# RWKV-7 head pairs: solver and preparation of the next pair moved into the running pair's chain, transposes over 128 partitions

## The chip, the core and the metric

The kernel runs on one core of a Trainium2 chip. The metric is the device time of one execution in microseconds (us), median of three runs. All matrix work runs on TensorE (PE), whose weight loads are listed apart (PEld); the elementwise work is spread over VectorE (DVE), ScalarE (ACT) and GpSimd (POOL), and SyncE (SP) issues the DMAs.

## What is computed

The program is a trunk of two layers. Each layer normalises x (512 tokens by 1024), projects it, runs four mixers on it (Mamba-2 SSD, RWKV-7, differential attention, grouped-query attention), projects their joined output back, normalises and adds. The change lies in the RWKV-7 mixer alone. Its core, per head and direction, is a recurrence over tokens:

```python
def step(S, inp):
    r_t, w_t, k_t, v_t, a_t, b_t = inp
    sa = jnp.einsum("bhvk,bhk->bhv", S, a_t)
    S = S * w_t[:, :, None, :] + sa[..., None] * b_t[:, :, None, :] + v_t[..., None] * k_t[:, :, None, :]
    return S, jnp.einsum("bhvk,bhk->bhv", S, r_t)
...
wkv = wkv_f + flip(wkv_b)
```

There are 8 heads of 64 channels, and one scan runs forwards and one backwards over the 512 tokens. Each layer also computes:

```python
mix = jnp.einsum("ble,ed->bld", jnp.concatenate([y_a, y_b, y_c, y_d], axis=-1), w_out[i])
x = x + _rms_norm(mix, post_norm_w[i])
```

## The kernel before

**Stages.** A layer runs in order: pre-norm and a low-rank projection; `prep(0)`, the preparation of the first head pair; the RWKV-7 stage with its four head pairs j; then SSD and the output projection. In the trace the RWKV-7 stage of the first layer is 100.5 to 676 us, that of the second 1019 to 1592 us.

**A head pair.** Two heads lie on the two halves of the 128 partitions. The 512 tokens are 8 chunks of 64; within a chunk the recurrence is solved as a 64x64 triangular system, and from chunk to chunk a 64x64 state is carried. Both directions d run side by side. The steps of a pair, in program order:
- `products(j)`: the 64x64 products of r and a against k and b (tile `pa`), masked into `AT` by DVE. Before, both m (k or b) are computed in one loop, and the two halves e go to output half `e ^ m`, so all four quadrants (input half by output half) of the PE array are used.
- `turned(j)`: V transposed by 64x64 products with the identity (`p`, line 82), and b with k transposed two at a time by PE (`pt`, line 452), evicted by ACT into `V2` and `BKT`.
- the solver: the 16x16 diagonal blocks of the system are brought side by side by four DVE stream transposes of 32 partitions by 512 (line 528), inverted in 15 steps of two small DVE instructions (lines 541, 543), and put back by eight more stream transposes (lines 549, 551) into `DN` and `DT`; three rounds of PE products with a DVE addition each (`ch`, `TT`, line 571) make the inverse `TT`.
- products that the chain needs: `px` (into `AT[0]`), `pk` (into `KV`) and `py` (the part of the output that needs no state, into `Y0`).
- the chain over 8 chunks, cc: from the state `St` the product `bk` row 0, then DVE adds `Xs`, then `bk` row 1 with `TT`, then DVE copies `Us`, then `bk` row 2 and DVE makes the new state `S`; outputs accumulate in the PSUM tile `yb`. These are three hops between PE and DVE in each chunk, 24 in a pair.
- `norm(j)`: group norm and gate of the finished pair.

**What goes in between.** `fill(us)` lets attention work (projections `pjt`, `pjc`, scores `sc`, softmax, `ptp`, `ob`) run in the amount of `us` times a scale that spends the same total in each layer. `ahead()` takes one step of a list of generators: `turned(j)`, `norm(j - 1)`, `prep(j + 1)`. Both are called between the solver's steps (`F_SV`, `F_MG`) and between the chain's hops (`F_CH`). `products(j + 1)` run inside the chain, from the fourth chunk on. A scheduler then orders the instructions of each engine; every engine works its own list in order.

The call that paces a hop of the chain, and the pacing scale, are:

```python
fill.scale = END * 299.5 / (4 * (15 * F_SV + 5 * F_MG + 24 * F_CH) + F_GN)
ahead()
fill(F_CH)
```

`prep(j)` (line 333 on) issues about 13 DVE instructions of 128x512 for each direction, the ACT exponentials and logarithms, and the small PE products `p`, among them `block_mm`, which has ACT make `bh` and POOL make `bl` first (lines 283, 284).

Of the kernel before, what the change touches and what calls it, by code (L numbers as in the profile page):

```python
# [10 lines left out]
F32 = mybir.dt.float32  # L11
# [8 lines left out]
L = 512  # L20
# [7 lines left out]
F_SV = 1.5  # L28
F_MG = 2.4
F_CH = 1.7  # L30
# [7 lines left out]
C_LAG = 4  # L38
N_PR = 3
# [36 lines left out]
def trunk(ctx: ExitStack, tc: tile.TileContext, x_in, win, wwd, wdt, wout, w2a, cols, rows, sscal, consts, out, dbg=None,  # L76
# [175 lines left out]
    def rwkv(i, lay, pw, ps, rp, fill):  # L252
# [63 lines left out]
        def prep(j):  # L316
# [18 lines left out]
            for d in range(2):  # L335
# [79 lines left out]
        BKT = rp.tile([128, 2, 2, 8, 64], F32, tag="BKT", name="BKT")  # L415
        V2 = rp.tile([128, 2, 8, 64], F32, tag="V2", name="V2")

        ba = AT[0][:, :, :, 0, :]
        half = [slice(0, 64), slice(64, 128)]

        def products(j, c0, n):

            ar = AR[:, j % 2:j % 2 + 3:2]
            for d in range(2):
                BK = sts[j]["BK"][d][:, 64:].rearrange("p (c a t) -> p c a t", c=8, a=2)
                pa = [ps.tile([128, n, 128], F32, tag="g", name="pa") for _ in range(2)]
# [5 lines left out]
                for m in range(2):
                    V.tensor_tensor(AT[m][:, d, c0:c0 + n].rearrange("p c a t -> p c (a t)"), pa[m],
                                    rmask.unsqueeze(1).to_broadcast([128, n, 128]), op=ALU.mult)

        def turned(j):
            BK, v = sts[j]["BK"], sts[j]["v"]
            for d in range(2):

                p5 = ps.tile([128, 8, 64], F32, tag="g", name="p5")  # L440
                for cc in range(8):
                    for e in range(2):
                        mm(p5[half[1 - e], cc, :], v[d][half[e], cc * 64:cc * 64 + 64], ident[half[e], half[e]], True, True)
                S.activation(V2[:, d], p5, AF.Copy)
                yield
            for d in range(2):
                for e in range(2):
                    pt = ps.tile([128, 8, 64], F32, tag="g", name="pt")

                    n = 7 + e  # L450
                    for cc in range(n):
                        PE.transpose(pt[:, cc, :], BK[d][half[e], (2 * cc + 1 - e) * 64:(2 * cc + 3 - e) * 64],
                                     ident[half[e], half[e]])
                    S.activation(BKT[:, d, e, 0:n], pt[:, 0:n], AF.Copy)
                    yield
# [47 lines left out]
        fill.scale = END * 299.5 / (4 * (15 * F_SV + 5 * F_MG + 24 * F_CH) + F_GN)  # L503
        products(0, 0, 4)
        products(0, 4, 4)
        ys = None
        for j in range(4):
            Aa, Ar, lamC = (sts[j][n] for n in ("a", "r", "lamC"))
            ahead.gens = [turned(j)]
# [7 lines left out]
            sv = rp.tile([128, 1024], F32, tag="sv", name="sv", bufs=1)  # L517
            As = sv[:, 0:512].rearrange("p (t s) -> p t s", t=16)
            As2 = sv[:, 512:768].rearrange("p (t s) -> p t s", t=16)
            Ti = sv[:, 768:1024].rearrange("p (t s) -> p t s", t=16)  # L520
            DT = rp.tile([128, 2, 8, 64], F32, tag="dt", name="DT", bufs=1)
            DN = rp.tile([128, 2, 8, 64], F32, tag="dn", name="DN", bufs=1)
            G.memset(sv[:, 768:1024], 0.0)
            G.memset(sv[:, 768:1024:17], 1.0)
            quad = [(slice(32 * q, 32 * q + 32), slice(32 * (q % 2), 32 * (q % 2) + 32)) for q in range(4)]
            unit = lambda t, q: t[quad[q][0], :, :, quad[q][1]].rearrange("p d c (h t) -> p t h (d c)", h=2)
            for q in range(4):
                V.transpose(out=As[quad[q][0]].rearrange("p t (h s) -> p t h s", h=2), in_=unit(ba, q))
            V.scalar_tensor_tensor(As2, As[:, :, 0:16], th[0], As[:, :, 16:32], op0=ALU.mult, op1=ALU.add)

            bam = AT[0].rearrange("p d c a t -> p (d c) a t")[:, :, 0, :]
            G.tensor_tensor(bam, bam, nomask.unsqueeze(1).to_broadcast([128, 16, 64]), op=ALU.mult)
            G.memset(DT, 0.0)
            G.memset(DN, 0.0)
            for jj in range(15):
                ahead()
                fill(F_SV)
                n = 15 - jj
                ot = rp.tile([128, 64], F32, tag="ot", name="ot", bufs=1)
                o3 = ot[:, 0:n * (jj + 1)].rearrange("p (a b) -> p a b", a=n)  # L540
                V.tensor_tensor(o3, As2[:, jj + 1:16, jj:jj + 1].to_broadcast([128, n, jj + 1]),
                                Ti[:, jj:jj + 1, 0:jj + 1].to_broadcast([128, n, jj + 1]), op=ALU.mult)
                V.tensor_tensor(Ti[:, jj + 1:16, 0:jj + 1], Ti[:, jj + 1:16, 0:jj + 1], o3, op=ALU.add)

            Dx = sv[:, 0:512].rearrange("p (t h s) -> p t h s", t=16, h=2)
            for h in range(2):
                V.tensor_scalar(Dx[:, :, h, :], Ti, th[h], None, op0=ALU.mult)
            for q in range(4):
                V.transpose(out=unit(DN, q), in_=Dx[quad[q][0]].rearrange("p t h s -> p s h t"))
            for q in range(4):  # L550
                V.transpose(out=unit(DT, q), in_=Dx[quad[q][0]])
            ahead()
            fill(F_MG)
            chd = lambda d: ps.tile([128, 8, 64], F32, tag=f"ch{d}", name=f"ch{d}")
            both = [(cc, e) for cc in range(8) for e in range(2)]

            Mp = rp.tile([128, 2, 8, 64], F32, tag="sv", name="Mp", bufs=1)
            for d in range(2):
                pm = chd(d)
                for cc, e in both:  # L560
                    mm(pm[half[e], cc, :], ba[half[e], d, cc, :], DN[half[e], d, cc, :], True, True)
                S.activation(Mp[:, d], pm, AF.Copy)
            TT = rp.tile([128, 2, 8, 64], F32, tag="dn", name="TT", bufs=1)
            for n in range(3):
                ahead()
                fill(F_MG)
# [865 lines left out]
```

## Time and profile before

| | us |
|---|---|
| median of three runs | 1852.17 (1848.23 to 1852.95) |
| profiled execution | 1854.4 |
| its span, first to last instruction | 1852.6 |
| PE busy in the span | 1642.2 (89%) |
| DVE busy | 1163.1 (63%) |
| ACT busy | 810.5 (44%) |
| POOL busy | 698.9 (38%) |

The mean granted TensorE clock is 0.939 of full speed. Read it stage by stage: PE busy and the other engines' busy time in each stretch, then what PE waits for. Durations come from the profiled execution; in the profile a matrix product of float32 operands appears as two records, and records overlap, so the time of a row of products is taken from start to start.

### The profile page before, as it was taken

How to read it: one execution, taken by the hardware profiler on the slowest of the kernel's cores; microseconds unless marked ns; L12 is line 12 of the kernel's file. 1: busy time of each engine (PE TensorE's matmuls, PEld its weight loads, DVE VectorE, ACT ScalarE, POOL GpSimd, SP SyncE). 2: the span in 40 equal slices, each digit the busy share in tenths (PEclk: the TensorE clock that was granted, in tenths of full speed). 3: DMA queues.
4: the chain of work that ended last, by engine and by line, in shares of the span. 5: the costliest groups of instructions: out<-in, count | busy, mean ns of one | idle time of the engine just before them, and what ended most of it. 6: DMA issues, size and time to landing. Idle time of an engine off the chain costs nothing. (4 is left out here: it accounts for less than half of the span.)

```text
span 1852.6 us, 35939 instructions
## 1 busy us (share of the span) xinstructions
PE 1642.2 (89%) x14616; PEld 1325.0 (72%) x14616; DVE 1163.1 (63%) x2426; ACT 810.5 (44%) x1566; POOL 698.9 (38%) x728
## 2 busy tenths in 40 slices
PE   7887989998988999988897799899889898999888
PEld 6576767776767877766785677687677677778666
DVE  4587586676665437886256865956856744378852
ACT  4644245435524255442346442563444242554431
POOL 4443233334242334543354332433432323345333
PEclk9898999999989999989999989999999899999899
DMA  4111101111001114122431111011110011231223
GB/s 152 60 40 39 35 24 42 49 41 44 26 24 47 42 54 135 64 73 88 134 104 52 32 39 36 29 37 50 37 44 30 24 47 36 81 112 53 86 86 114
DMA packets 57510, 108.41 MB, mean 59 GB/s; under 512 B 6784, under 2 KB 8832, under 8 KB 57344
## 3 DMA queue, kind: packets, MB, share of 16 engines
q1 hardware_dynamic: 57344, 106.11, 17.7%
q8 instruction: 114, 1.87, 0.4%
q14 instruction: 52, 0.43, 0.1%
HBM read 95.60 MB, written 10.49 MB: 57 GB/s over the span
## 5 line engine op out<-in xcount | busy, mean ns | idle before, releaser
L144 POOL TENSOR_TENSOR wlo<-wf,whi 128x512 fp32r<-128x512 f32 x228 | 315.6, 1389 | 444.7 <-ACT whi L143 360.2
L82 PE MATMUL pjt<-whi,hhi 128*128 128x256 f32 x960 | 297.5, 310 | 13.0 <-ACT raw L269 6.5
L82 PE MATMUL pjt<-wlo,hhi 128*128 128x256 f32 x960 | 293.7, 307 | 1.1 <-POOL wlo L144 1.1
L82 PE MATMUL pjt<-whi,hlo 128*128 128x256 f32 x960 | 287.9, 300 | 0.0
L143 ACT ACTIVATE whi<-wf 128x512 fp32r<-128x512 f32 x228 | 141.3, 628 | 215.8 <-PE pjt L82 104.0
L82 PEld LDWEIGHTS pjt<-whi,hhi 128*128 128x128 f32 x960 | 192.6, 201 | 34.6 <-issue 9.0
L82 PEld LDWEIGHTS pjt<-wlo,hhi 128*128 128x128 f32 x960 | 192.6, 201 | 11.4 <-issue 6.5
L82 PEld LDWEIGHTS pjt<-whi,hlo 128*128 128x128 f32 x960 | 193.0, 201 | 8.8 <-issue 5.6
L82 PE MATMUL pjc<-hhi,whi 128*128 128x512 f32 x384 | 161.8, 421 | 9.0 <-ACT raw L269 5.2
L82 PE MATMUL pjc<-hhi,wlo 128*128 128x512 f32 x384 | 159.7, 418 | 0.0
L82 PE MATMUL pjc<-hlo,whi 128*128 128x512 f32 x384 | 158.1, 412 | 0.0
L872 DVE TENSOR_REDUCE nm<-sc 128x1 f32<-128x512 f32 x96 | 65.9, 687 | 84.6 <-PE sc L82 78.1
L875 ACT ACTIVATE p<-sc,nm 128x512 f32<-128x512 f32 x96 | 65.9, 686 | 115.1 <-DVE nm L872 114.7
L82 PE MATMUL mix<-whi,ylo 128*128 128x512 f32 x256 | 106.1, 414 | 5.4 <-DVE ylo L1216 5.4
L82 PE MATMUL sc<-qT,qT 64*128 64x512 f32 (+1 forms) x256 | 101.7, 494 | 7.2 <-ACT y L1055 3.8
L82 PE MATMUL mix<-whi,yhi 128*128 128x512 f32 x256 | 101.0, 417 | 5.1 <-ACT yhi L1215 5.1
L82 PE MATMUL mix<-wlo,yhi 128*128 128x512 f32 x256 | 104.4, 408 | 0.0
L82 PEld LDWEIGHTS pjc<-hhi,whi 128*128 128x128 f32 x384 | 76.5, 199 | 32.9 <-issue 6.6
L82 PEld LDWEIGHTS pjc<-hhi,wlo 128*128 128x128 f32 x384 | 76.3, 199 | 21.4 <-issue 4.2
L82 PEld LDWEIGHTS pjc<-hlo,whi 128*128 128x128 f32 x384 | 76.5, 199 | 15.7 <-issue 0.3
L1224 POOL TENSOR_TENSOR wlo<-wf,whi 128x512 fp32r<-128x512 f32 x32 | 44.4, 1390 | 112.3 <-ACT whi L1223 107.6
L1223 ACT ACTIVATE whi<-wf 128x512 fp32r<-128x512 f32 x64 | 40.4, 631 | 94.0 <-PE mix L82 59.3
(331 smaller groups left out, 3828.6 us busy)
## 6 DMA issues: line engine op xcount, KB each, us to landing
wf<-in_win_dram SPq DMA_DIRECT2D x224, 256.0 KB, 2.9
wf<-in_wout_dram SPq DMA_DIRECT2D x64, 256.0 KB, 2.6
y<-y_dram SPq DMA_DIRECT2D x24, 256.0 KB, 2.7
xt<-in_x_dram SPq DMA_DIRECT2D x8, 512.0 KB, 4.0
y_dram<-y SPq DMA_DIRECT2D x16, 256.0 KB, 2.7
y_dram<-rs SPq DMA_DIRECT2D x8, 256.0 KB, 2.1
x_dram<-t SPq DMA_DIRECT2D x8, 256.0 KB, 2.4
xt<-x_dram SPq DMA_DIRECT2D x4, 512.0 KB, 4.3
```

Source lines behind the costliest of these rows:

```text
L82: PE.matmul(o, lhsT, rhs, start=start, stop=stop, skip_group_check=skip)
L143: S.activation(hi, wf, AF.Copy)
L144: G.tensor_tensor(lo, wf, hi.bitcast(F32), op=ALU.subtract)
L872: V.tensor_reduce(nm, sc, axis=AX, op=ALU.max, negate=True)
L875: S.activation(p, sc, AF.Exp, bias=nm, accum_out=sm)
L1223: S.activation(hi, wf, AF.Copy)
L1224: (V if kt % 2 else G).tensor_tensor(lo, wf, hi.bitcast(F32), op=ALU.subtract)
```

## The change

It does these things in the RWKV-7 stage; nothing else in the program is changed.
- `solve(j)` is a generator of 31 steps that holds the products with b of pair j, the solver, and the transposes of V and k. `solve(0)` runs by itself after `prep(0)`. For j of 1 to 3 it follows `prep(j)` in the list of `ahead`, so that it runs inside the chain of pair j - 1. `ahead(2 + (n == 0))` takes two or three steps a hop.
- `bulk(j)` (12 steps) stands between the chains: the products with k, `px`, the transposes of b (`BT`), `KV`, and the part of the output that needs no state, which now accumulates into `yb` directly. `Y0` and `py` fall away, and `ys` becomes an ACT copy.
- All 64x64 products read and write the same half, so that two of the four quadrants are used. V, k and b are each transposed by 64x64 products with the identity, 768 in the program in place of 256 for V and 240 `pt` transposes.
- The stream transposes: four ACT copies bring the blocks into one tile, one DVE stream transpose of 128x512 turns it, three times a pair in place of twelve of 32x512. Over the program that is 96 of 32x512 out, 24 of 128x512 and 96 ACT copies of 32x512 in. The evictions of `pa` are all 128x512, 64 of them, in place of 88 of mixed sizes.
- The pacing constants: `F_SV` 0.7, `F_BU` 0.8, `F_CH` 2.3, `F_C3` 3.0 (last pair), with the same total.

The core of the diff:

```diff
-F_SV = 1.5
-F_MG = 2.4
-F_CH = 1.7
+F_SV = 0.7
+F_BU = 0.8
+F_CH = 2.3
+F_C3 = 3.0
...
+        quad = [(slice(32 * q, 32 * q + 32), slice(32 * (q % 2), 32 * (q % 2) + 32)) for q in range(4)]
+        unit = lambda t, q: t[quad[q][0], :, :, quad[q][1]].rearrange("p d c (h t) -> p t h (d c)", h=2)
+        both = [(cc, e) for cc in range(8) for e in range(2)]
+        bank = lambda nm: ps.tile([128, 8, 64], F32, tag="g", name=nm)
+        clear = lambda o: mm(o, cr[:, 272:273].to_broadcast([128, 128]), hT["hi"][:, 0, :], True, True)
+        rev = lambda d, cc: slice((7 * d + (1 - 2 * d) * cc) * 64, (7 * d + (1 - 2 * d) * cc) * 64 + 64)
+
+        def products(j, m):
 
             ar = AR[:, j % 2:j % 2 + 3:2]
+            to = AT[(j + m) % 2]
             for d in range(2):
+                BK = sts[j]["BK"][d]
+                for c0 in (0, 4):
+                    pa = ps.tile([128, 4, 128], F32, tag="g", name="pa")
+                    for cc in range(4):
                         for e in range(2):
+                            mm(pa[half[e], cc, :].rearrange("p (a t) -> p a t", a=2), BK[half[e], c0 + cc, m, :],
                                ar[half[e], :, d, c0 + cc, :], True, True)
...
+        def turned(src, to, d):
+
+            pt = bank("pt")
+            for cc, e in both:
+                mm(pt[half[e], cc, :], src(cc)[half[e]], ident[half[e], half[e]], True, True)
+            S.activation(to[:, d], pt, AF.Copy)
...
+        def solve(j):
+            yield from products(j, 0)
+            s = sts[j]
+            ba = AT[j % 2][:, :, :, 0, :]
+            sv = rp.tile([128, 1024], F32, tag="sv", name="sv", bufs=1)
+            As = sv[:, 0:512].rearrange("p (t s) -> p t s", t=16)
+            As2 = sv[:, 512:768].rearrange("p (t s) -> p t s", t=16)
+            Ti = sv[:, 768:1024].rearrange("p (t s) -> p t s", t=16)
+            DT = rp.tile([128, 2, 8, 64], F32, tag="dt", name="DT", bufs=1)
+            DN = rp.tile([128, 2, 8, 64], F32, tag="dn", name="DN", bufs=2)
+            s["TT"] = DN
+            close = DT[:, 0].rearrange("p c t -> p (c t)")
+            G.memset(DN, 0.0)
+            thu = lambda t, q: t[quad[q][0]].rearrange("p (t h u) -> p t h u", t=16, h=2)
+            for q in range(4):
+                S.activation(thu(close, q), unit(ba, q), AF.Copy)
+            yield
+            V.transpose(out=sv[:, 0:512], in_=close)
+            V.scalar_tensor_tensor(As2, As[:, :, 0:16], th[0], As[:, :, 16:32], op0=ALU.mult, op1=ALU.add)
+            G.memset(sv[:, 768:1024], 0.0)
+            G.memset(sv[:, 768:1024:17], 1.0)
+            G.memset(DT, 0.0)
...
+            for to, view in ((DN, "p t h s -> p s h t"), (DT, None)):
+                close = sv[:, 512:1024]
+                V.transpose(out=close.rearrange("p (t h s) -> p t h s", t=16, h=2), in_=Dx.rearrange(view) if view else Dx)
+                for q in range(4):
+                    S.activation(unit(to, q), thu(close, q), AF.Copy)
+                yield
...
+            s["V"] = rp.tile([128, 2, 8, 64], F32, tag="sv", name="VT", bufs=1)
+            s["K"] = rp.tile([128, 2, 8, 64], F32, tag="dt", name="KT", bufs=1)
+                turned(lambda cc: s["v"][d][:, cc * 64:cc * 64 + 64], s["V"], d)
+                yield
+                turned(lambda cc: s["BK"][d][:, cc, 1, :], s["K"], d)
+                yield
...
+        def bulk(j):
+            s = sts[j]
+            VT, KT, ba, ka = s["V"], s["K"], AT[j % 2][:, :, :, 0, :], AT[1 - j % 2]
+            yield from products(j, 1)
+            for d in range(2):
+                px = bank("px")
+                for cc, e in both:
+                    mm(px[half[e], cc, :], ka[half[e], d, cc, 0, :], VT[half[e], d, cc, :], True, True)
+                S.activation(ba[:, d], px, AF.Copy)
+                yield
+            for d in range(2):
+                turned(lambda cc: s["BK"][d][:, cc, 0, :], BT, d)
+                yield
+            s["KV"] = KV = rp.tile([128, 2, 8, 64], F32, tag="kv", name="KV", bufs=1)
+            for d in range(2):
+                pk = bank("pk")
+                for cc, e in both[:14]:
+                    mm(pk[half[e], cc, :], KT[half[e], d, cc, :], VT[half[e], d, cc, :], True, True)
+                V.tensor_tensor(KV[:, d, 0:7], pk[:, 0:7, :], s["lamC"][:, d, 0:7].unsqueeze(2).to_broadcast([128, 7, 64]),
+                                op=ALU.mult)
+                yield
+            s["yb"] = yb = ps.tile([128, L], F32, tag="yb", name="yb")
+            clear(yb)
+            for d in range(2):
+                for cc, e in both:
+                    mm(yb[half[e], rev(d, cc)], VT[half[e], d, cc, :], ka[half[e], d, cc, 1, ::1 - 2 * d], False, True, True)
+                yield
...
-        fill.scale = END * 299.5 / (4 * (15 * F_SV + 5 * F_MG + 24 * F_CH) + F_GN)
-        products(0, 0, 4)
-        products(0, 4, 4)
+        fill.scale = END * 299.5 / (30 * F_SV + 48 * F_BU + 72 * F_CH + 24 * F_C3 + F_GN)
+        for _ in solve(0):
+            fill(F_SV)
...
+            for _ in bulk(j):
+                fill(F_BU)
...
-                ahead.gens.append(prep(j + 1))
+                ahead.gens += [prep(j + 1), solve(j + 1)]
+            def step(n):
+                ahead(2 + (n == 0))
+                fill(F_CH if j < 3 else F_C3)
...
-            V.tensor_tensor(ys, yb, Y0, op=ALU.add)
+            S.activation(ys, yb, AF.Copy)
```

DVE while the inverse of the first pair is finished, before (`thw`, `lr`, `cs`, `AR`, `rn`, `lk`, `b`, `BK`, `rk` are prep(1); `DN`, `DT` and `sv` the solver):

```order
L549 STREAM_TRANSPOSE DN<-sv 32x16x2x16 x2
L347 TENSOR_SCALAR thw<-thw 128x512
L261 SCALAR_TENSOR_TENSOR lr<-raw,cols,lt 128x512
L353 SCALAR_TENSOR_TENSOR cs<-cst,thw 128x128 x4
L549 STREAM_TRANSPOSE DN<-sv 32x16x2x16 x2
L551 STREAM_TRANSPOSE DT<-sv 32x16x2x16 x4
L375 TENSOR_TENSOR AR<-lr,lam 128x512
L374 SCALAR_TENSOR_TENSOR rn<-lk,cols,rn 128x512
L384 TENSOR_TENSOR lk<-ka,lk 128x512
L387 TENSOR_TENSOR AR<-rn,lam 128x512
```

The same place of the changed kernel (`solve(0)`; `nm`, `rs`, `r`, `p` are the softmax of attention, `KV` belongs to `bulk(0)`):

```order
L483 TENSOR_SCALAR sv<-sv,cst 128x16x16 x2
L486 STREAM_TRANSPOSE sv<-sv 128x512
L862 TENSOR_REDUCE nm<-sc 128x1
L486 STREAM_TRANSPOSE sv<-sv 128x512
L867 RECIPROCAL rs<-sm 128x1
L1021 SCALAR_TENSOR_TENSOR r_1418<-rs,nlam,sm 128x1
L1022 SCALAR_TENSOR_TENSOR p<-p,r_1418 128x512
L503 TENSOR_TENSOR DN<-ph,DT 128x512 x6
L433 TENSOR_TENSOR AT_435<-pa,cst 128x512 x4
L532 TENSOR_TENSOR KV<-pk,lamC 128x448 x2
```

No instruction of prep(1) stands here any more; eight transposes have become two.

DVE in the first pair's chain, around the second chunk, before (`Xs`, `Us`, `S` are the chain):

```order
L389 SCALAR_TENSOR_TENSOR b_1838<-tha,rn 128x512
L384 TENSOR_TENSOR lk<-ka,lk 128x512
L872 TENSOR_REDUCE nm<-sc 128x1
L390 SCALAR_TENSOR_TENSOR BK<-b_1838,il 128x8x64
L624 TENSOR_TENSOR Xs_1788<-bk_1769,AT_434 128x64
L624 TENSOR_TENSOR Xs_1792<-bk_1772,AT_434 128x64
L877 RECIPROCAL rs<-sm 128x1
L263 SCALAR_TENSOR_TENSOR lv<-raw,cols,lt 128x512
L1031 SCALAR_TENSOR_TENSOR r_1705<-rs,nlam,sm 128x1
L635 COPY Us_1815<-bk_1769 128x64
```

The same chunk of the changed kernel:

```order
L1022 SCALAR_TENSOR_TENSOR p<-p,r_1677 128x512
L374 TENSOR_TENSOR AR<-lr,lam 128x512
L373 SCALAR_TENSOR_TENSOR rn<-lk,cols,rn 128x512
L381 TENSOR_TENSOR lk<-ka,lk 128x512
L384 TENSOR_TENSOR AR<-rn,lam 128x512
L386 SCALAR_TENSOR_TENSOR b_1804<-tha,rn 128x512
L387 SCALAR_TENSOR_TENSOR BK<-b_1804,il 128x8x64
L397 SCALAR_TENSOR_TENSOR rk<-lr,cols,lk 128x512
L260 SCALAR_TENSOR_TENSOR lv<-raw,cols,lt 128x512
L262 SCALAR_TENSOR_TENSOR lk<-raw,cols,lt 128x512
L308 SCALAR_TENSOR_TENSOR gate<-gate,pjc 128x512
L626 COPY Us_1919<-bk_1792 128x64
```

Ten instructions of prep(1) that stood ahead of the chain, and some behind its first chunk, now stand in a row between this chunk's `Xs` and its `Us`.

## Rows read from the trace of the kernel before

**Rows 1.** Windows, RWKV-7 stage of both layers: start:end, length, busy us (instructions) of PE, PEld, DVE, ACT, POOL, then granted clock, DMA share, GB/s.

```profile
100.50:676.00 575.50, 516.94 (x5775) 416.01 (x5774) 372.31 (x839) 245.02 (x483) 195.57 (x190) 0.94 0.12 37
1019.00:1592.00 573.00, 515.57 (x5765) 416.20 (x5764) 371.20 (x837) 243.30 (x479) 194.27 (x189) 0.93 0.12 37
```

**Rows 2.** Windows, first layer: four solver stretches, two of four chains, sum of all eight.

```profile
113.30:173.40 60.10, 47.35 (x661) 37.95 (x660) 49.27 (x81) 31.01 (x50) 17.84 (x21) 0.89 0.10 32
...
237.50:320.20 82.70, 73.01 (x822) 58.12 (x820) 64.05 (x124) 45.53 (x81) 32.77 (x28) 0.96 0.11 34
320.20:385.50 65.30, 64.38 (x664) 49.63 (x665) 38.30 (x99) 25.97 (x50) 21.65 (x25) 1.00 0.15 48
385.50:467.40 81.90, 69.52 (x807) 58.19 (x803) 60.57 (x103) 40.27 (x69) 33.59 (x27) 0.92 0.12 40
467.40:545.80 78.40, 70.55 (x707) 56.55 (x710) 50.90 (x143) 31.03 (x78) 26.29 (x29) 0.91 0.09 28
545.80:619.40 73.60, 66.45 (x832) 55.57 (x830) 37.78 (x80) 31.74 (x69) 17.89 (x16) 0.95 0.11 37
...
sum 559.80, PE 502.22 PEld 404.41 DVE 364.67 ACT 240.63 POOL 187.90; mean PE 62.78 PEld 50.55 DVE 45.58 ACT 30.08 POOL 23.49
```

**Rows 3.** Waits of PE in 100.5 to 676 us: in total us, times, longest.

```profile
PE p L82 <- ACT bh L283: 15.4, 4, 10.9
PE bk L82 <- DVE Xs L624: 8.4, 2, 4.5
```

**Rows 4.** Timeline around the longest wait: start, us, engine, instruction, count [idle before].

```profile
137.83 4.30 DVE L551 STREAM_TRANSPOSE DT<-sv 32x512 f32<-32x512 f32 x4
...
142.16 0.69 DVE L375 TENSOR_TENSOR AR<-lr,lam 128x512 f32<-128x512 f32 x1
...
150.64 0.80 PE L82 MATMUL p<-bh,cr 128*128 128x512 f32 x1 [10.94 <-ACT bh L283]
```

**Rows 5.** Timeline in the third pair's chain.

```profile
522.69 5.52 DVE L997 SCALAR_TENSOR_TENSOR gqk<-gqk,grr,arow 128x128 f32<-128x128 f32 x12 [2.06 <-POOL grr L126]
...
529.08 0.48 PE L82 MATMUL bk<-Xs,TT 64*64 64x64 f32 x4 [4.50 <-DVE Xs L624]
```

**Rows 6.** Window just behind the longest wait.

```profile
150.60:155.00 4.40, 4.36 (x16) 1.86 (x18) 2.07 (x3) 3.05 (x6) 2.66 (x4) 0.50 0.15 51
```

**Rows 7.** Groups of DVE instructions, whole program: count, busy us, mean ns.

```profile
L549 DVE STREAM_TRANSPOSE DN<-sv 32x512 f32<-32x512 f32 x32 | 38.7, 1209 | 1.3 <-DVE sv L547 0.5
L551 DVE STREAM_TRANSPOSE DT<-sv 32x512 f32<-32x512 f32 x32 | 34.4, 1074 | 0.6
L528 DVE STREAM_TRANSPOSE sv<-AT 32x512 f32<-32x512 f32 x32 | 33.8, 1057 | 0.4
...
L715 DVE TENSOR_TENSOR su<-su,sdt 64x512 f32<-64x512 f32 x2 | 1.4, 682 | 0.0
```

**Rows 8.** Groups of ACT instructions, whole program.

```profile
L258 ACT ACTIVATE lt<-raw,dv 128x512 f32<-128x512 f32 x52 | 37.3, 720 | 26.3 <-DVE BK L390 12.8 <-DVE lk L384 7.7 <-POOL bl L284 3.2
...
L444 ACT ACTIVATE V<-p 128x512 f32<-128x512 f32 x16 | 9.5, 596 | 28.5 <-PE p L82 28.5
```

**Rows 9.** Timeline of PE: transposes of V, then of b and k.

```profile
113.33 2.08 PE L82 MATMUL p<-cst,lv 64*64 64x64 f32 x64
...
116.35 0.95 PE L452 MATMUL pt<-cst,BK 64*128 64x64 f32 x15
```

**Rows 10.** Timeline of PE: pa in four quadrants, in two.

```profile
106.53 1.37 PE L82 MATMUL pa<-AR,BK 64*64 64x128 f32 x32
...
238.06 0.65 PE L82 MATMUL pa<-AR,BK 64*64 64x128 f32 x8
...
499.78 1.10 PE L82 MATMUL pa<-AR,BK 64*64 64x128 f32 x32
```

**Rows 11.** Group of PE instructions that clear py, whole program.

```profile
L82 PE MATMUL py<-hhi,cr 128*128 128x512 f32 x8 | 4.0, 499 | 0.2
```

More of the change, by code (lines that the diff above doesn't have):

```diff
@@ L431, in products @@
                                ar[half[e], :, d, c0 + cc, :], True, True)
[L432 to L437, printed above, removed]
-            for d in range(2):
[L440 to L444, printed above, removed]
+                    V.tensor_tensor(to[:, d, c0:c0 + 4].rearrange("p c a t -> p c (a t)"), pa,
+                                    rmask.unsqueeze(1).to_broadcast([128, 4, 128]), op=ALU.mult)
@@ L523, in rwkv @@
[L523 to L566, printed above, removed]
-                for d in range(2):
-                    ph = chd(d)
-                    for cc, e in both:
-                        mm(ph[half[e], cc, :], Mp[half[e], d, cc, :], (TT if n else DT)[half[e], d, cc, :], True, True)
-                    V.tensor_tensor(TT[:, d], ph, DT[:, d], op=ALU.add)
@@ L588, in rwkv @@
-            py = ps.tile([128, L], F32, tag="g", name="py")
-            clear = lambda o: mm(o, cr[:, 272:273].to_broadcast([128, 128]), hT["hi"][:, 0, :], True, True)
-            rev = lambda d, cc: slice((7 * d + (1 - 2 * d) * cc) * 64, (7 * d + (1 - 2 * d) * cc) * 64 + 64)
-            clear(py)
-            for d in range(2):
-                for cc, e in both:
-                    mm(py[half[e], rev(d, cc)], V2[half[1 - e], d, cc, :], AT[1][half[1 - e], d, cc, 1, ::1 - 2 * d],
-                       False, True, True)
@@ L596, in rwkv @@
-            S.activation(Y0, py, AF.Copy)
-            made = 0
-            yb = ps.tile([128, L], F32, tag="yb", name="yb")
-            clear(yb)
+                ahead.gens += [prep(j + 1), solve(j + 1)]
+            def step(n):
+                ahead(2 + (n == 0))
+                fill(F_CH if j < 3 else F_C3)
             St = [None, None]
             for cc in range(8):
-                if cc >= C_LAG:
-                    ahead.finish()
-                if j < 3 and not ahead.gens and cc - made >= N_PR:
-                    n = min(4, cc - made)
-                    products(j + 1, made, n)
-                    made += n
-                bks = []
+                bks = [ps.tile([128, 8, 64], F32, tag=f"ch{d}", name=f"bk{d}") for d in range(2)]
@@ L611, in rwkv @@
                 for d in range(2):
[L612 to L613 removed]
                     if cc:
                         for e in range(2):
[L616 to L618 removed]
+                            mm(bks[d][half[e], 0, :], Aa[half[e], d, cc, :], St[d][half[e], :], True, True)
+                step(0)
@@ L644, in rwkv @@
                             mm(yb[half[e], rev(d, cc)], St[d][half[e], :], Ar[half[e], d, cc, ::1 - 2 * d], False, True, True)
-                        mm(yb[half[e], rev(d, cc)], Us[half[e]], AT[0][half[e], d, cc, 1, ::1 - 2 * d], False, True, True)
+                        mm(yb[half[e], rev(d, cc)], Us[half[e]], br[half[e], d, cc, ::1 - 2 * d], False, True, True)
                     if cc < 7:
                         St[d] = Sn
-                ahead()
-                fill(F_CH)
+                step(2)
             ahead.finish()
-            while j < 3 and made < 8:
-                n = min(4, 8 - made)
-                products(j + 1, made, n)
-                made += n
             ys = rp.tile([128, L], F32, tag="tmp", name="ys", bufs=3)
-            V.tensor_tensor(ys, yb, Y0, op=ALU.add)
+            S.activation(ys, yb, AF.Copy)
         for _ in norm(3, ys):
```

107 lines of the change are left out of this document (43 added, 64 removed).

## The prediction

> **What bounds the kernel now.** I read the windows of the RWKV-7 stage first. In each layer PE is busy 517 of 575 us and DVE 372 [rows 1], so PE sets the pace and its idle time, 58 us a layer (575.5 - 516.9; 573.0 - 515.6), is what a reordering can win. The finer windows say where it lies [rows 2]: in the four stretches that hold a solver PE idles 12.8 + 9.7 + 12.4 + 7.2 = 42 us, and in all eight 559.8 - 502.2 = 57.6, so the four chains hold the other 15.6. The list of PE's waits names the largest: 15.4 us for `bh`, 10.9 of it in one wait [rows 3]. The timeline shows how that one comes about: DVE turns `DT` for 4.3 us, then works through prep(1), and PE stands for 10.94 us until ACT has `bh` of prep's `rk` [rows 4]. So it is not the solver's chain that is late there but prep(1) behind the solver's lumps on DVE's list. The second entry, `bk` for `Xs`, is of another kind: 4.50 us behind twelve rotations of attention, 5.52 us in a row on DVE [rows 5].
>
> [...]
>
> **DVE and ACT.** Out go 96 stream transposes of 32x512, 38.7 + 34.4 + 33.8 = 106.9 us; in come 24 of 128x512. No row shows one. If an instruction is paid by its elements per partition, each costs what 32x512 does, 1.06 us [rows 7]; if by 32 partitions at a time, four times that, 4.2; the floor is the 0.68 of a 512-wide addition [rows 7]. I take 1.06, since an addition of 64x512 costs 0.682 and a two-operand product of 128x512 0.69 [rows 4, 7]: partitions cost nothing there. That is 25 us (16 to 101), net -81 over the program, some 41 us a layer. ACT takes 96 copies for it, at 0.60 (plain copy) to 0.72 us [rows 8], strided as they are: 58 to 69 us, or +29 to 35 a layer on an engine with 245 of 575 busy. They are priced at nothing for the span where the solver runs inside a chain, with five or more hops to spare; in `solve(0)` they are in line.
>
> **PE.** Three terms, over both layers.
> - The identity products: those of V stay, b and k need 512 where 240 transposes stood. A 64x64 product is two records, and 64 records took 2.08 us [rows 9], about 29 ns each after the first, so 512 x 0.059 = 30 us; a `pt` transpose took 0.95 / 15 = 0.063 us, 15 us in all. Net **+15**.
> - `pa`: 1024 records, as before. Where four quadrants alternate a record took (1.10 - 0.27) / 31 = 27 ns, or 35 in other places; where only two ran, (0.65 - 0.27) / 7 = 54 [rows 10] (0.27 is one record's own duration). The changed kernel uses two always. From about 35: 1024 x 0.019 = **+20**. Bounds: 28 from the faster row, 0 if the lone row of two is no rule.
> - The eight products that clear `py`: **-4** [rows 11].
>
> Sum +31 us, and it is paid in full only where PE isn't waiting anyway.
>
> [...]
>
> **Idle time.** The move takes prep and the solver out of each other's way: what was in the solver stretches, 42 us a layer, goes, the 10.94 us with it. What is late next, stretch by stretch:
> - `solve(0)` has no chain beside it and no prep. Its bounds are the 12.8 us of the first solver stretch [rows 2] and the 1.8 that are left there without the wait for `bh`. Its 30 fills of 0.7 (times the scale of 0.93) are 19 us of cover for copies, transposes, 15 DVE steps and the rounds. I take 7.
> - The chains 0 to 2 now have the solver and prep on DVE's list between `Xs`, `Us` and `S`, and whatever stands ahead of these holds PE. Counting the changed order at the durations of this trace I get for DVE and PE, in us of an estimate, 62 beside 70 in chain 0, 64 beside 83 in chain 1, 87 beside 94 in chain 2, 38 beside 68 in chain 3, and PE almost alone in `bulk`. What such a load costs shows in the windows of before as idle over PE's busy time: 11% at a ratio of 0.72 (467.4), 13% at 0.88 and 18% at 0.87 (237.5, 385.5), 27% at 1.04 (113.3), 1% at 0.59 (320.2), 11% at 0.57 (545.8) [rows 2]. The windows over 0.8 had their twelve transposes in lumps of two to four, which are gone, so I go below them: 10, 8, 14 and 4 us, ends 5 to 11, 4 to 9, 8 to 21 and 1 to 7.
> - The steps of `bulk` depend on one another but have little DVE: 2 us.
>
> Together 45 us a layer in place of 58, **-26**. The rotations' wait [rows 5] is in it: they stay on DVE's list, somewhere in chains 2 and 3.
>
> [...]
>
> **Sum.** 1854.4 (profiled) + 31 - 26 - 14 = 1845. The profile lies 2.2 us over the median of 1852.17, so by the median **1843**, 0.5% faster. POOL loses 16 memsets and no DMA moves past another; both are taken at nothing, with POOL at 196 of 575 us [rows 1].
>
> **The rivals.**
> - *DVE's list becomes the bound in chains 0 to 2* (slower). The order shows it: ten instructions of prep in a row between an `Xs` and an `Us`. It has 72 hops a layer to work on. Before, a chain's hop lost 15.6 / 96 = 0.16 us; my forecast has about 0.44. Break-even with the +31 and the clock is near 0.5, idle of 48 us a layer. At 0.65 us a hop idle is 47 + 13 = 60, +4 over both layers, the clock gives nothing back, and the time is 1854.4 + 31 + 4 - 2.2 = 1887; half way there, 1870. For it: the ratio of 0.92 in chain 2, and the wait of 4.50 us that a single lump made. Against: the solver's steps are short, and PE's fill lies ahead of each hop. A transpose of 4.2 us would lead here too.
> - *The waits are attention's and prep's own and only change place* (the change doesn't do what it says). Of the idle time only the 10.94 us and a few near it go, 11 a layer: 31 - 22 - 6 of clock = +3, so 1855, no change.
> - *Small waits don't lower the clock and `pa` isn't dearer.* The window 320.2 shows what a chain with little idle gets: clock 1.00. With `pa` as before (+11 for PE), idle of 38 a layer (-40) and 10 of clock a layer (-20): 1854.4 + 11 - 40 - 20 - 2.2 = 1803. With `pa` at its price and idle of 35, near 1815.
>
> **How the numbers follow.** A difference of under 0.3% (1846.6 to 1857.7) can't be told from none. The forecast has 0.40, as 1828 to 1857 (0.28 faster, 0.12 same); the first rival 0.26, from 1860 to 1890 (slower); waits that only move 0.12 (0.02 faster, 0.05 same, 0.05 slower); the fast one 0.22 (faster). That makes 0.52 faster, 0.17 same, 0.31 slower. Leaving out a tenth at each end, the range is 1803 to 1880.
>
> **What would show it.** PE's idle time of 100 to 676 us near 45 in place of 58; no wait of 10 us for `bh`; the 128x512 transposes near 1.06 us; PE's records of `pa` near 54 ns apart; waits of PE for `Xs`, `Us`, `S` and `bh` spread over the chains in pieces of under 3 us; the stage's clock at 0.95 or better. I am wrong if chain 0 or 2 shows idle over 20%, if `solve(0)` stands for over 12 us, or if PE's busy time doesn't rise.

## The result, and the profile after

The changed kernel takes 1904.37 us (median of four runs, 1895.91 to 1909.41); the kernel before took 1852.56 beside it. The ratio is 1.028 with an interval of 1.0235 to 1.0322: slower by 2.8%, outside the predicted range of 1803 to 1880. The profiled execution, at 1895.91, is the fastest of the four, so the profile shows 41 of the 52 us lost. Of all executions that follow, the ratios leave out one disturbed one, of 5067 us, among the ten of `a_line_cc`.

| us | before | after | difference |
|---|---|---|---|
| span | 1852.6 | 1893.9 | +41.3 |
| PE busy | 1642.2 | 1680.3 | +38.1 |
| rest of the span, PE idle | 210.4 | 213.6 | +3.2 |
| DVE busy | 1163.1 | 1071.7 | -91.4 |
| ACT busy | 810.5 | 917.1 | +106.6 |
| mean granted clock | 0.939 | 0.943 | |

The stage in windows, as in [rows 1] but up to SSD's first product (start:end, length, busy of PE, PEld, DVE, ACT, POOL, clock, DMA share, GB/s), of the first layer before:

```profile
100.60:693.20 592.60, 532.82 (x5889) 429.97 (x5888) 376.86 (x851) 257.43 (x506) 202.84 (x201) 0.94 0.12 38
```

and of both layers after:

```profile
101.55:710.70 609.15, 549.88 (x6254) 445.02 (x6254) 331.72 (x795) 307.92 (x548) 201.76 (x191) 0.94 0.11 37
...
1040.30:1649.50 609.20, 549.76 (x6255) 444.97 (x6254) 331.89 (x795) 308.02 (x548) 202.44 (x191) 0.94 0.11 37
```

PE idles 59 us in each, as against 60 before, and is 17 us longer busy. DVE is down by 45 us a layer (41 were forecast), ACT up by some 50, where 29 to 35 were forecast. In finer windows of the first layer (`solve(0)` with `bulk(0)`, then chain 0, `bulk(1)`, chain 1, and so on to chain 3 and what follows it), for [rows 2]:

```profile
101.60:172.00 70.40, 61.19 (x959) 53.87 (x958) 32.17 (x67) 33.25 (x53) 19.20 (x16) 0.93 0.09 30
172.00:254.80 82.80, 74.47 (x601) 54.41 (x601) 64.39 (x155) 43.66 (x67) 33.24 (x33) 0.94 0.12 39
254.80:311.00 56.20, 52.27 (x845) 44.04 (x839) 24.42 (x47) 28.45 (x52) 9.39 (x9) 0.97 0.05 14
311.00:401.60 90.60, 82.48 (x737) 62.63 (x735) 64.53 (x151) 56.06 (x87) 39.59 (x39) 0.98 0.15 52
401.60:443.00 41.40, 39.71 (x754) 36.79 (x750) 12.54 (x25) 14.78 (x28) 7.87 (x9) 0.96 0.08 28
443.00:564.00 121.00, 106.63 (x1017) 81.61 (x1017) 77.25 (x193) 70.14 (x128) 42.98 (x35) 0.87 0.09 32
564.00:605.00 41.00, 35.32 (x518) 28.83 (x512) 14.12 (x30) 13.97 (x28) 7.93 (x10) 0.92 0.04 15
605.00:689.00 84.00, 77.69 (x715) 65.63 (x714) 37.02 (x115) 33.05 (x82) 33.10 (x35) 0.96 0.17 57
689.00:710.70 21.70, 20.06 (x142) 17.15 (x140) 5.27 (x14) 14.52 (x28) 8.40 (x8) 1.00 0.18 63
```

The waits of PE in 101.6 to 710.7 us, for [rows 3] (in total us, times, longest):

```profile
PE ob L81 <- ACT ptS L889: 7.6, 5, 2.2
PE sc L81 <- DVE qT L903: 6.6, 2, 5.9
PE bk L81 <- DVE S L636: 6.3, 4, 3.7
PE pqt L898 <- DVE gqk L920: 5.6, 1, 5.6
...
PE pm L81 <- ACT DN L488: 3.4, 5, 1.4
PE p L81 <- ACT bh L282: 2.6, 1, 2.6
```

The 10.94 us for `bh` are gone. In their place stand waits of attention for what ACT and DVE owe it (`ptS`, `qT`, `gqk`). Summed over the whole list, 32 us of waits end on DVE, 19 on ACT and 8 on POOL; before they were 33, 23 and 5 (100.6 to 693.2 us). So the waits have new owners and nearly the old sum. The longest of them, in `solve(0)`:

```profile
117.04 0.62 ACT L902 ACTIVATE qT<-pqt 128x512 fp32r<-128x512 f32 x1
...
124.48 0.68 DVE L903 SCALAR_TENSOR_TENSOR qT<-pqt,qT 128x512 fp32r<-128x512 f32 x1
...
125.22 1.22 PE L81 MATMUL sc<-qT,qT 64*128 64x512 f32 x2 [5.94 <-DVE qT L903]
```

ACT has done its part of `qT` at 117.7, but DVE's part stands behind the solver's small steps, which fill DVE's list from 117.7 to 124.5. The timeline just behind the first chain shows how the largest group arises, as [rows 4] did before:

```profile
257.56 0.66 PE L887 MATMUL ptp<-cst,p 128*128 128x128 f32 x4
...
258.45 4.39 ACT L488 ACTIVATE DT<-sv 32x512 f32<-32x512 f32 x4
262.87 0.60 ACT L889 ACTIVATE ptS<-ptp 128x512 f32<-128x512 f32 x1
...
263.51 0.76 PE L81 MATMUL ob<-v,ptS 128*128 128x128 f32 x3 [2.13 <-ACT ptS L889]
```

Attention's `ptp` is done at 258.2, but ACT works through four of the solver's copies first, and then `Mp`'s two stand behind `ptS`. The four copies take 4.39 us. The groups for [rows 7] and [rows 8] (count, busy us, mean ns):

```profile
L461 ACT ACTIVATE DT<-AT 32x512 f32<-32x512 f32 x32 | 35.3, 1104 | 8.0 <-DVE AT L433 7.6
L488 ACT ACTIVATE DN<-sv 32x512 f32<-32x512 f32 x32 | 34.9, 1092 | 5.7 <-DVE sv L486 5.3
L488 ACT ACTIVATE DT<-sv 32x512 f32<-32x512 f32 x32 | 34.6, 1082 | 0.9 <-DVE sv L486 0.4
...
L486 DVE STREAM_TRANSPOSE sv<-sv 128x512 f32<-128x512 f32 x16 | 14.4, 902 | 20.4 <-ACT DN L488 20.2
L463 DVE STREAM_TRANSPOSE sv<-DT 128x512 f32<-128x512 f32 x8 | 5.7, 711 | 19.5 <-ACT DT L461 19.5
```

A copy costs 1.09 us, not 0.60: the work has gone from one engine's list to the other's, and a DVE transpose of 0.71 to 1.11 us comes on top (902 ns is the mean of `DN`'s and `DT`'s):

```profile
L486 DVE STREAM_TRANSPOSE sv<-sv x16: 712/893/1109, 129.5 to 1480.0; 128x512 f32<-128x512 f32 x16
```

Here 712/893/1109 are the shortest, the median and the longest in ns. PE's own terms came as forecast. Its timeline, for [rows 9] and [rows 10]:

```profile
151.79 3.84 PE L81 MATMUL pa<-AR,BK 64*64 64x128 f32 x64
...
158.21 2.03 PE L81 MATMUL pt<-cst,BK 64*64 64x64 f32 x64
```

That is (3.84 - 0.27) / 63 = 57 ns a record of `pa`, and 29 ns a record of the transposes. Over the program `pa` takes PE 80.5 us in place of 60.6.

### The profile page after: what moved, and what is told of

Same layout as the page of the kernel before. It is cut to its first block, busy times and chain, and to the rows that moved or that the text cites. A ratio compares the mean times of both kernels' runs of the same rounds, so it can differ in the third digit from the quotient of the medians.

```text
span 1893.9 us, 37439 instructions
## 1 busy us (share of the span) xinstructions
PE 1680.3 (89%) x15392; PEld 1356.6 (72%) x15392; DVE 1071.7 (57%) x2322; ACT 917.1 (48%) x1662; POOL 696.4 (37%) x712
## 5 line engine op out<-in xcount | busy, mean ns | idle before, releaser
L143 POOL TENSOR_TENSOR wlo<-wf,whi 128x512 fp32r<-128x512 f32 x228 | 321.7, 1416 | 576.6 <-ACT whi L142 548.1
L81 PE MATMUL pjt<-whi,hhi 128*128 128x256 f32 x960 | 291.7, 304 | 15.0 <-ACT raw L268 7.5
L81 PE MATMUL pjt<-wlo,hhi 128*128 128x256 f32 x960 | 285.5, 298 | 1.1 <-POOL wlo L143 1.1
L81 PEld LDWEIGHTS pjt<-whi,hhi 128*128 128x128 f32 x960 | 188.4, 196 | 31.2 <-ACT raw L268 8.8
L81 PEld LDWEIGHTS pjt<-wlo,hhi 128*128 128x128 f32 x960 | 188.7, 197 | 11.5 <-issue 8.3
L81 PEld LDWEIGHTS pjt<-whi,hlo 128*128 128x128 f32 x960 | 188.6, 196 | 5.2 <-issue 3.0
L81 PE MATMUL ob<-v,ptS 128*128 128x128 f32 x512 | 78.2, 299 | 15.6 <-ACT ptS L889 15.1
L81 PEld LDWEIGHTS ob<-v,ptS 128*128 128x128 f32 x512 | 67.1, 203 | 26.0 <-ACT ptS L889 24.3
```

Of the source, the lines that this page charges most:

```text
L81: PE.matmul(o, lhsT, rhs, start=start, stop=stop, skip_group_check=skip)
L143: G.tensor_tensor(lo, wf, hi.bitcast(F32), op=ALU.subtract)
```

## Experiments

Three causes stood to choice: the added work of TensorE (A), waits made by the new order (B), and the copies on ACT's list (L). Ratios are to the kernel before on the same chip. Where the intervals of two variants overlap, their difference is not clear, and the text says so.

**TensorE's work, in the old order.** `b_diag`:

```diff
-mm(pa[m][half[e ^ m], cc, :]...
+mm(pa[m][half[e], cc, :]...
```

> The kernel before with one edit: all pa products go to the output half that equals their input half, so two quadrants of the array run in place of four. The k half of the result lands on the wrong half of the partitions, so the output is not the reference's; number and size of all instructions are unchanged. Theory A (the loss is added TensorE work): pa's busy time rises by 20 us over the program as it did in the changed kernel (52.8 to 75.5), and the time by as much, to about 1873. Theory B (the loss is waiting, made by the solver inside the chain): pa's 20 us are hidden in waits, the time stays within 5 us of 1852. [...]

Measured 1864.36, ratio 1.0064 (1.0046 to 1.0081): +12 us, between the two expectations. The time of `pa` alone (a window over the whole span, that tile's instructions; behind the length stand PE and PEld) rose by 24, and PE's busy time as a whole by 13, from 1642.2 to 1655.1:

```profile
0.00:1852.60 1852.60, 60.64 (x1024) 42.18 (x1024) 44.65 (x88) 0.94 0.18 59
```

```profile
0.00:1862.10 1862.10, 84.35 (x1024) 65.75 (x1024) 44.76 (x88) 0.94 0.19 58
```

So the second of these, with row halves that alternate as in the first, shows `pa` dearer in two quadrants, 84.35 us in place of 60.64. By the same count the changed kernel's is 80.51; no view here shows the expectation's 52.8 and 75.5.

`b_copy` replaces the twelve 32x512 transposes of the kernel before by `S.activation(thu(close, q), unit(ba, q), AF.Copy)` and the like, as the diff has them.

> The kernel before with the stream transposes alone changed: twelve ACT copies and three 128x512 DVE transposes for a pair in place of twelve 32x512 DVE transposes, in the same places. DVE should lose about 88 us of busy time and ACT gain 105 (1.09 us a copy in the changed kernel). Theory A: TensorE's work is the same, the waits move, the time is within 10 us of 1852. A third theory, T (the lumps of DVE transposes made the waits of the solver stretch, as the prediction had it): the 10.9 us wait for bh shrinks by half or more in each layer and the time falls by 10 to 25 us, to 1827 to 1842.

1850.96, ratio 1.0007 (0.9981 to 1.0033): nothing, where 10 to 25 us of gain were the other expectation. The lump on DVE is gone, and waits for ACT have come; PE's list of 100 to 690 us has

```profile
PE ch L82 <- ACT Mp L566: 7.3, 2, 4.3
...
PE p L82 <- ACT rs L469: 5.7, 1, 5.7
PE pt L452 <- ACT V L444: 3.9, 2, 2.2
PE ptp L901 <- DVE p L1036: 3.5, 6, 1.1
PE p L82 <- ACT bh L283: 3.1, 3, 2.4
```

`b_all` is both, and

```diff
-PE.transpose(pt[:, cc, :], BK[d][half[e], (2 * cc + 1 - e) * 64:(2 * cc + 3 - e) * 64], ...)
+for b in range(2):
+    lo = (2 * cc + 1 - e + b) * 64
+    mm(pt[half[b], cc, :], BK[d][half[e], lo:lo + 64], ident[half[e], half[e]], True, True)
```

> The kernel before, in its old order, with the three pieces of work of the changed kernel: pa on two quadrants (as b_diag, the output is not the reference's), the copies with 128x512 transposes (b_copy), and b and k transposed by 64x64 products with the identity, 480 in place of 240 transposes. Alone the first cost 12 us and the second nothing. Theory A (added work is the loss): 12 and up to 15 for the transposes and more where they meet, 1875 to 1895, most of the way to 1904. Theory B (the new order is the loss): 1852 + 12 + at most 15, so 1860 to 1880, and the remaining 25 to 40 us are the order's.

1876.66, ratio 1.0128 (1.0109 to 1.0147). The work of the changed kernel costs 25 us in the old order, about half of the loss; the time lies in the ranges of A and of B alike.

**The same work taken away, in the new order.** `a_quad` writes the second half of the chunks to the other output half, alternating:

```diff
+pas = [ps.tile([128, 4, 128], F32, tag="g", name="pa") for _ in range(2)]
+for cc in range(4):
+    for b in range(2):
+        for e in range(2):
+            mm(pas[b][half[e ^ b], cc, :]..., BK[half[e], 4 * b + cc, m, :], ar[half[e], :, d, 4 * b + cc, :], ...)
```

> The changed kernel with one edit: the two halves of the chunks of pa are computed alternately, the second half to the other output half, so that all four quadrants run again. The second half of the chunks is then exchanged between the two heads, so the output is not the reference's. Theory A: pa falls by 20 us or more, the time from 1904 to about 1884. Theory B: within 6 us of 1904.

1900.64, ratio 1.0269 (1.0215 to 1.0324), not to be told from the changed kernel's. PE's busy time fell from 1680.3 to 1663.5, and its idle time rose from 213.6 to 230.9: in the new order that work had been filling waits, as B expects. `a_work` is `a_quad` with `for cc, e in both[:2 * n]`, n = 4 for k and b:

> The changed kernel, in its new order, with TensorE's work brought down to that of before: pa on four quadrants as in a_quad, and only half of the products that transpose k and b (256 of 512; the other half of the tiles is filled with copies of the first). The output is not the reference's. TensorE then has about 35 us less to do than in the changed kernel. Theory A: back to 1860 to 1872. Theory B: what is saved turns into waits, 1885 to 1900; a_quad, where 17 us of saved work became 17 us of idle time, points this way.

1891.37, ratio 1.0237 (1.0197 to 1.0277), in B's range: 13 us under the changed kernel by the medians, 8 by the ratios, and not clear of its interval. PE's busy time fell by 23 and its idle time rose by 15. So work added to the old order costs its 25 us, and work taken out of the new order gives little of it back: neither A nor B holds alone.

**The copies.** `a_dvet` puts the twelve DVE transposes back into the new order:

> The changed kernel with the twelve 32x512 DVE transposes for a pair again, without the ACT copies; all else as changed. DVE gains about 85 us of busy time, ACT loses 105. Theory A: TensorE's work is the same, time within 10 us of 1904. Theory B, in the form that DVE's list binds the chains: slower by 15 to 40 us, 1920 to 1945. If it is ACT that is overloaded by copies of 1.09 us (twice what was taken for them): faster by 10 to 20, 1884 to 1894.

1916.04, ratio 1.033 (1.0284 to 1.0376), 12 us over the changed kernel by the medians, but the intervals overlap; it lies in none of the three ranges. So in the new order the copies cost about what the transposes cost that they replaced. `a_cc` leaves all instructions in place but makes the copies contiguous:

```diff
-S.activation(thu(close, q), unit(ba, q), AF.Copy)
+S.activation(close[quad[q][0]], AT[j % 2][quad[q][0]].rearrange("p d c a t -> p (d c a t)")[:, 0:512], AF.Copy)
...
-S.activation(unit(to, q), thu(close, q), AF.Copy)
+S.activation(to[quad[q][0], q % 2].rearrange("p c t -> p (c t)"), close[quad[q][0]], AF.Copy)
```

> The changed kernel with the 96 ACT copies of 32x512 reading and writing contiguous elements in place of the strided, regrouped ones; the values that the solver then gets are not the system's, so the output is not the reference's. Number, size, engine and place of all instructions are unchanged. If stride is what makes a copy take 1.09 us, it falls to about 0.60 and ACT loses 45 us of busy time. Theory L (the copies on ACT's list hold up attention, 34 us of idle a layer against 25 before): attention's idle falls towards 25 a layer and the time by 12 to 25 us, to 1880 to 1892. Theory A (only TensorE's work counts): within 6 us of 1904.

1879.39, ratio 1.0155 (1.0111 to 1.0198): -25 us. The same three groups of ACT, on `a_cc`:

```profile
L488 ACT ACTIVATE DN<-sv 32x512 f32<-32x512 f32 x32 | 20.1, 628 | 25.0 <-DVE sv L486 24.5
L461 ACT ACTIVATE DT<-AT 32x512 f32<-32x512 f32 x32 | 20.1, 627 | 7.2 <-DVE AT L433 6.8
L488 ACT ACTIVATE DT<-sv 32x512 f32<-32x512 f32 x32 | 20.1, 627 | 0.8 <-DVE sv L486 0.4
```

and of PE's waits in 101.6 to 710 us:

```profile
PE bk L81 <- DVE Us L626: 8.9, 5, 3.3
PE ob L81 <- ACT ptS L889: 2.0, 3, 1.5
PE pm L81 <- ACT DN L488: 0.3, 1, 0.3
```

`ptS`, which only stands on the same list as the copies, is waited for 2.0 us in place of 7.6. In exchange the chain waits longer for DVE (`Us`, 8.9 in place of 1.9). Over the program PE idles 199.4 us in place of 213.6, in the slowest of the four executions. One thing besides stride is changed: a contiguous copy reads and writes other elements, so that a reader can need fewer of the four copies (`DN` is waited for 0.3 us in place of 3.4). What share of the 25 us that has wasn't tested.

`a_mix` splits: the first four and `DN` on DVE, `DT` by copies.

> The changed kernel with the transposes of b_mix: the first four and DN by 32x512 DVE transposes, DT by one 128x512 transpose and four copies; ACT has 32 strided copies in place of 96, DVE 64 transposes of 32x512 in place of none. If the series of copies ahead of DN is what costs the changed kernel its 25 us (a_cc 1879), this gives most of it: 1875 to 1888. If in the new order DVE's list is as full as ACT's (a_dvet with 96 on DVE took 1916), the two balance: 1895 to 1912.

1932.93, ratio 1.0443 (1.0391 to 1.0495), above both ranges and the worst of all. PE idles 216.2 us, hardly more than the changed kernel's 213.6, but it is busy 1714.2 in place of 1680.3, at a granted clock of 0.919 in place of 0.943. Busy time times clock is nearly the same, 1575 and 1585 us, so what is lost here goes with the clock. Why it is slower than `a_dvet`, with fewer transposes on DVE, stays open.

**The order.** `a_line`:

```diff
+for _ in solve(j):
+    fill(F_SV)
 for _ in bulk(j):
     fill(F_BU)
...
-ahead.gens += [prep(j + 1), solve(j + 1)]
+ahead.gens += [prep(j + 1)]
...
-ahead(2 + (n == 0))
+ahead()
```

> The changed kernel with the solver of each pair taken out of the chain: it runs alone between two chains, as solve(0) does, paced with 1.0 a step; the chain has prep and norm beside it, one step a hop, paced with 1.6; the total of the fill is the same. Work is unchanged. Theory A: within 8 us of 1904. Theory B (the solver's steps on the lists of DVE and ACT hold up the chain, and its tail holds up what follows): the chains lose idle time, 1875 to 1890. If slower than 1915, it is the solver's own latency that wants the chain as cover.

1886.87, ratio 1.0196 (1.0159 to 1.0234): -17 us. But `a_line` changes the pacing too (`F_SV` 1.0, `F_CH` and `F_C3` 1.6). Another pacing alone, with the solver left in the chain, is `a_ch` (`F_BU` 0.3, `F_CH` 2.63):

> The changed kernel with another split of the same total of fill: bulk 0.3 a step in place of 0.8, the chain's hops of the first three pairs 2.63 in place of 2.3. Theory B: the hops have more cover, 1885 to 1900. If the steps of bulk wait for each other more than the chain does, 1910 to 1925. Theory A: within 8 us of 1904.

1889.43, ratio 1.02 (1.0185 to 1.0215): -15, nearly as much. So the 17 us of `a_line` can't be put down to the solver's place: place and pacing aren't separated. The lower `F_BU` in `a_line2` (`F_BU` 0.3, `F_SV` 1.2) gave no gain:

> a_line (solver out of the chain) with the split of the fill that helped in a_ch: bulk 0.3 a step in place of 0.8, the solver's steps 1.2 in place of 1.0, same total. If what is left between a_line (1887) and the old order with the same work (b_all, 1877) is the pacing of bulk, it comes to 1873 to 1880; if it is the order of bulk itself, it stays within 6 us of 1887.

1899.54, ratio 1.0244 (1.0209 to 1.0278), 13 us above `a_line` by the medians, with intervals that overlap; neither of the two expectations. `a_line_cc` joins `a_line` and `a_cc`:

> a_line (solver out of the chain) with the contiguous copies of a_cc; the output is not the reference's. If the loss by the solver inside the chain (1904 against 1887) is the strided copies on ACT's list beside the chain, then out of the chain they cost less: gain under 12 us, 1875 to 1887. If the copies cost the same 25 us out of the chain, where they stand in the solver's own line, 1858 to 1868, and the two losses add.

1846.87, ratio 0.9978 (0.9957 to 1.0): 40 us under `a_line` and below both ranges. The copies cost out of the chain as well, where they stand in the solver's own line, and more than the 25 expected. Since its values are not the system's, two kernels with right values asked the same. `a_line_mix`:

> a_line (solver out of the chain) with the transposes of b_mix: the first four and DN by 32x512 DVE transposes, DT by one 128x512 transpose and four copies. In the chain the same transposes cost 29 us (a_mix 1933 against 1904). If DVE's list was too full only there, they gain out of it: 1858 to 1875. If a_line_cc's 1847 came from its values and not from its shorter copies, this stays within 8 us of 1887.

1879.29, ratio 1.0159 (1.0132 to 1.0186), 8 us under `a_line`, at the edge of what was to count as nothing, with intervals that overlap. And `a_line_dvet`:

> a_line with all twelve 32x512 DVE transposes and no copies. Same question: 1860 to 1880 if DVE has room out of the chain, within 8 us of 1887 or above if not.

1870.1, ratio 1.0125 (1.0057 to 1.0193), in the range expected if DVE has room out of the chain: 46 us under `a_dvet`, which has the same transposes inside it. Under `a_line` it lies by 17, but the intervals overlap. That points the same way as `a_line_cc`; whether the values of `a_line_cc` have a share in the other 23 us stays open.

**A better kernel.** `b_copy` had shown the lump gone and the solver's line longer. `b_mix`, in the old order, changes `DT` alone, which is needed last:

```diff
-for q in range(4):
-    V.transpose(out=unit(DT, q), in_=Dx[quad[q][0]])
+close = sv[:, 512:1024]
+V.transpose(out=close.rearrange("p (t h s) -> p t h s", t=16, h=2), in_=Dx)
+for q in range(4):
+    S.activation(unit(DT, q), thu(close, q), AF.Copy)
```

> The kernel before with the change of the transposes made only for DT, which is needed later than DN: one 128x512 DVE transpose and four ACT copies in place of four 32x512 DVE transposes; DN and the first four stay as they were. In b_copy the wait for bh fell from 19 to 9 us a layer but the solver's own waits rose from 4 to 18, as its next product stood behind copies of 1.09 us in series. Theory L: here the lump on DVE gets 3.4 us shorter without that series ahead of DN, so 1838 to 1848. Theory A: within 5 us of 1852.

1821.35, ratio 0.983 (0.9804 to 0.9856): 1.7% faster than before, more than expected. PE idles 190.3 us in place of 210.4 and is busy 1630.5 in place of 1642.2, at a clock of 0.949 against 0.939. The stretch of [rows 4] in it:

```profile
138.03 0.71 DVE L552 STREAM_TRANSPOSE sv<-sv 128x512 f32<-128x512 f32 x1
...
138.78 4.39 ACT L554 ACTIVATE DT<-sv 32x512 f32<-32x512 f32 x4
...
145.57 0.48 PE L82 MATMUL ch<-DT,Mp 64*64 64x64 f32 x4 [4.50 <-ACT Mp L565]
146.08 0.80 PE L82 MATMUL p<-bh,cr 128*128 128x512 f32 x1
```

0.71 us on DVE in place of 4.30: `p` starts 4.6 us earlier, at 146.08, and waits no longer for `bh` but for ACT's `Mp` ahead of it, which the copies delay. `b_mix2` also makes the first transposes by copies:

> b_mix with the first four transposes of a pair also made by four copies and one 128x512 transpose; only DN keeps the 32x512 DVE transposes. The first ones have nothing to hide behind: the copies take 4 x 1.09 us in line where the transposes took 4 x 1.06. If only the lump behind the inverse counts: within 6 us of 1821. If DVE's list as a whole counts, 1810 to 1816; if each series of copies in the solver's line costs as in b_copy, 1828 to 1838.

1832.76, ratio 0.9886 (0.9859 to 0.9914): 11 us of the gain are lost again, as expected if a series of copies in the solver's line costs. `b_best` is `b_mix` with `yb` accumulating the stateless part:

> b_mix, and the part of the output that needs no state accumulated straight into yb, as in the changed kernel: eight clears of TensorE, eight DVE additions and the tile Y0 fall away. 4 us of TensorE's work less (0.50 us a clear): 3 to 5 us under b_mix by theory A, 1835 to 1845 with theory L's gain; if yb's clear then waits for the copy of the pair before, no gain.

1824.54, ratio 0.9849 (0.9812 to 0.9886), the same as `b_mix`.

## Why the prediction was wrong

In the profiled execution the sum comes out 50 us too low. Idle time has 29 of it (+3 in place of -26), PE's busy time the other 21 (+38 in place of +31 for its work and -14 for the clock).

- **PE's work, +31: right in size.** Busy time rose by 38.1; `pa` at 57 ns a record (+20 us, as worked out) and the identity products at 29 came as forecast. In the old order they cost 25 us (`b_all`). In the new order only part of that shows, since PE waits anyway (its idle time rose by 15 us in `a_work`, 17 in `a_quad`); the prediction had said that the sum is paid in full only where PE isn't waiting.
- **DVE, -81: right** (-87 for the transposes, -91 in all). The 128x512 transpose took 0.71 to 1.11 us, where 1.06 was taken.
- **ACT "priced at nothing for the span": the step that failed first.** A copy was taken at 0.60 to 0.72 us, from rows of contiguous access; it took 1.09. And the copies were not off the path: four in a row are 4.4 us, in which attention's `ptS` and the solver's own next step stand still. Contiguous copies give back 25 us (`a_cc`), 40 out of the chain (`a_line_cc`); both kernels compute other values, and readers can need fewer of their copies.
- **Idle time 45 us a layer, -26: the term that missed by most; it stayed 59.** The step was that the idle time of the solver stretches, 42 us a layer, goes. The wait for `bh` went, and others came (above). The chains came near their forecast: 8.3, 8.1, 14.4 and 6.3 us against 10, 8, 14 and 4, and `solve(0)` with `bulk(0)` 9.2 against 7 and a share of 2. What was missed is `bulk`, put at 2 us in all and with 3.9, 1.7 and 5.7 between the chains alone, where the tail of the solver and the waits of attention fell: 5.6 of the 5.7 are one wait for `gqk`, the tile of [rows 5], which the forecast had counted in the chains. 1.6 us more lie behind chain 3, which the forecast left out.
- **Clock, -14: no run shows this term of the sum.** It is the author's estimate, as are the 6 and the 20 us of clock in two of the rivals; the trace of before shows a clock of 0.50 for 4.4 us behind the longest wait [rows 6]. In the changed kernel that wait is gone, others of 5.9 and 5.6 us stand in its place, the idle time didn't fall, and the stage's clock is 0.94 as before. In `b_mix`, with 20 us less idle time, the clock was 0.949 in place of 0.939 and PE was busy 12 us less.
- **The mechanism ahead of it was right, in the old order.** Shortening the lump of DVE transposes ahead of prep(1) gave 32 us (`b_mix`); but not all copies could take the lump's place for free (`b_copy`, nothing).
- **The rivals.** The first, DVE's list bound in the chains, at 1870 to 1887, was nearest in time, but not by its mechanism: the chains idle what the forecast had for them. The second, waits that only change place, has the mechanism that the idle time shows, with nothing won in place of 11 us a layer; its 1855 was 49 us too low. A kernel with the solver in the chain is 17 us slower than one without it with the copies (`a_line`), 46 with DVE transposes (1916 against 1870), the pacing being changed with it. The losses are not additive: 25 for work, 25 for the contiguous copies and 17 for chain and pacing exceed the 52 measured.
- **The signs that the prediction named.** None that it is wrong came: chains 0 and 2 idle 11% and 13% over PE's busy time, `solve(0)` with `bulk(0)` 9.2 us, and PE's busy time rose. Three that it is right stayed out: idle time near 45, waits of the chain in pieces of under 3 us (3.7 for `S`), a clock of 0.95. None of the signs of being wrong looked at ACT or at what `bulk` waits for.

With contiguous copies and the solver out of the chain the time is 1847 (`a_line_cc`, with other values and another pacing), next to the forecast of 1843. How the loss divides between the copies, the place of the solver, the pacing and the clock stays open.

## What to carry to other kernels

An engine with half its time free still has a list: ACT was busy for 48% of the span here, and four copies of 4.39 us ahead of `ptS` made PE stand for 2.13 us. Price an instruction that is moved to such an engine by its access pattern (a copy took 1.09 us regrouped, 0.63 contiguous), and ask who stands behind it. Of a group of steps moved off a crowded engine, move only those whose result is needed late; moving all of them brought nothing here, moving a third of them 1.7%. And count a hop of a chain between two engines as cover for another chain on the same engines only after looking at what else stands on their lists: here it gave nothing.

## What the hardware showed that was not expected

- The price of an instruction went with its access pattern, on both engines. ACT copies of 32x512: contiguous 0.63 us (`a_cc`), regrouped 1.09, 1.7 times as long. DVE stream transposes: 0.71 us for 128x512 where both sides are contiguous, about 1.1 where the read is regrouped (`DN`); 1.06 to 1.07 for 32x512 with one side hopping at every element, 1.21 with both, which is 1.5 and 1.7 times the 0.71. So the 1.06 of [rows 7] had very likely been stride. That is an estimate from these times; a contiguous 32x512 transpose was not run.
- The clock didn't follow the sum of the waits alone: the changed kernel, `a_dvet` and `a_mix` leave PE idle for 214, 212 and 216 us, at clocks of 0.943, 0.924 and 0.919, and PE is busy 27 and 34 us longer in the second and third. The executions of one kernel differ as well, 0.931 to 0.943 for the changed one, but those of `a_mix` lie below that, at 0.910 to 0.926. What makes the difference isn't shown.
